# Sums of squares of queries and keys by two transfers of ScalarE instead of four of SyncE, and the first gates of the MLPs over both token runs side by side

## The chip, the cores and the metric

The kernel runs on one core of one Trainium2 chip. The metric is the device time of one execution in microseconds (us). TensorE (PE) multiplies matrices, with a weight load (PEld) beside each product; VectorE (DVE), ScalarE (ACT) and GpSimd (POOL) work on vectors; SyncE (SP) does nothing here but issue transfers (DMAs). An engine runs its instructions in their order: one that waits holds up all that stand behind it on that engine. ACT and POOL can issue transfers too, between their other instructions.

## The reference

A decoder of two layers over 528 tokens (16 learned ones ahead of 512), width 1024. Layer 0 is attention with a forget gate, layer 1 a gated linear recurrence (HGRN2), and each is followed by a gated MLP. What bears on the change:

```python
q, k, v, f_logit, o_gate = split(rms_norm(h) @ w_in)
q = rms_norm(q.reshape(B, L, 16, 64), q_gain) * 64 ** -0.5
k = rms_norm(k.reshape(B, L, 16, 64), k_gain)
p = softmax(where(causal, q . k + c_t - c_s, -inf))
o = (p @ v) * sigmoid(o_gate)
...
a = rms_norm(h) @ w_gate
a = conv_b + conv_w[0] * a[t - 2] + conv_w[1] * a[t - 1] + conv_w[2] * a[t]
y = (silu(a) * (rms_norm(h) @ w_up)) @ w_down
```

The mean squares in the change's name are those of `rms_norm(q)` and `rms_norm(k)`, one number for each token and head.

## The kernel before

Activations lie transposed, features on the partitions and tokens along the row, and the 528 tokens are cut into two runs of 264 (`full`). A product is made to float32 accuracy out of three products of halves: `proj_unit` gives for each tile of 128 features high weights by high input (L255), high weights by low input (L258), low weights by high input (L259). `weights` brings a 128x1024 block of weights by one SP transfer (L199), makes its high half on ACT (`hi`, L200) and its low half on DVE (`lo`, L126).

The program names what each engine has to do in Python generators (`fox` for the attention, `hgrn`, `ffn` for the MLPs), which `weave` steps in turn by the costs that they yield. A scheduler of the framework then orders the instructions of each engine by a simulated timeline, and puts in the waits. So an edit in one place can shift the order around it on every engine.

The attention (`fox`) goes over eight pairs of heads. In one iteration four pairs are in work: `stage_a` of pair p+3, `stage_n` of p+2, `lse` of p+1, and the attending itself of pair p.

- `stage_a` projects queries and keys. ACT squares the sums (L540) and copies them scaled (L541). A product with `hsel` adds the squares over each head (L549), two heads by four groups of (query or key) by (run), into one bank. ACT copies it to `strow` (L550). Four SP transfers (L554) fold the eight rows of `strow` into `am2`, 64 partitions by 33, on which DVE works quickly: it adds `et`, the epsilon term of every token (L557), and takes the inverse root in ten operations (L343 to L347). Two transfers (L564) unfold the result into `rows`.
- `stage_n` spreads `rows` over the partitions with the table `sel` (L578, PE), multiplies queries and keys by it (L579, DVE), makes high and low halves, and packs them by six SP transfers a pair (`pack`, L605) into `pk` or `two`; `decays` adds rows of the forget gate by SP (L617).
- `lse` finds the softmax's maxima and sums, two heads a pair: scores on PE (L751, L752, L754), maxima on DVE (L764 to L772), sums on ACT (L119, `junk`), and the row `lrow` (L786 on PE, L788 on DVE, transfers L791 and L792).
- The attending makes the scores again (L808, L809), probabilities `pt` on ACT (L119), and their product with `v` (L823). In between PE does projections, the output gate's and the values' among them (L306 and others). Vector `tot` (L486) of the forget gate is needed by L488.

Ahead of the pairs, `et` is filled by four SP transfers (L440) from `ssr`, the mean squares of the tokens, which two equal rows hold.

In the MLPs `plain(j)` works on the first two blocks of 128 gates, m = 0 and 1, with the plain products (later blocks use another scheme). `ga` names its two token runs: (0, 264) and (264, 264) in the first MLP, (14, 256) and (270, 258) in the second. For each run `proj_unit` goes over eight tiles, and DVE multiplies the bank by the tokens' inverse norms into `A` (L1256).

```python
am2 = self.tiny.tile([64, 33], F32, name="am2", tag="am2")
for g in range(4):
    nc.sync.dma_start(
        am2[16 * g : 16 * g + 16, :], strow[32 * g : 32 * g + 2, :].rearrange("r (j c) -> r j c", c=33)
    )
nc.vector.tensor_tensor(am2, am2, et, ALU.add)
```

## Time and profile before

| | us |
| --- | --- |
| median of three runs (lowest to highest) | 1445.19 (1443.09 to 1445.87) |
| the profiled execution, its own time | 1447.99 |
| span of the profiled execution | 1446.2 |
| PE busy in it | 1417.7 |
| DVE busy | 1009.4 |
| ACT busy | 723.9 |

The profiled execution is 1.8 us above its span and 2.8 us above the median. PE is busy for 98% of the span, so the time is set by what PE has to do, by the clock that it is granted, and by the 28.5 us in which it does nothing. A row of a timeline gives start, duration and instruction, and in brackets the idle time just before it and what ended it. The attention lasts until some 376 us, the first MLP starts at 377 us, the second near 1110 us.

### The profile page before, as it was taken

What the parts mean: (1) busy time and instruction counts of PE and PEld (TensorE: products, weight loads), DVE (VectorE), ACT (ScalarE), POOL (GpSimd) and SP (SyncE); (2) the same over time, 40 slices, a digit from 0 to 9 for tenths busy, and PEclk for the clock granted to TensorE, in tenths of its full rate; (3) what the DMA queues carried; (4) which work ended last, traced back from release to release, by engine and by line L of the source; (5) the groups of instructions that cost most, each with busy time, mean ns of one, the idle gap of its engine ahead of it and who ended that gap; (6) DMA issues with size and microseconds to landing.
All of it is one profiled execution on the core that took longest, in us unless ns stands there. A gap on an engine that the chain in (4) does not pass through costs nothing.

```text
span 1446.2 us, 29795 instructions
## 1 busy us (share of the span) xinstructions
PE 1417.7 (98%) x11368; PEld 1336.7 (92%) x11368; DVE 1009.4 (70%) x2282; ACT 723.9 (50%) x1528; POOL 178.7 (12%) x309
## 2 busy tenths in 40 slices
PE   7999999999999999999999999999999999999998
PEld 7898878999999999999999999999999899999997
DVE  6546454776698876777776667687567887777774
ACT  5355555664566555454543323333345665555551
POOL 4000000000412222221000000000022222222100
PEclk9999999999999999999999999999999999999999
DMA  4424344422889898896321202212165899989733
GB/s 162 121 63 134 67 126 124 111 86 85 225 184 253 217 227 212 204 221 152 95 77 60 88 19 71 74 60 73 60 182 138 217 251 224 233 214 224 200 89 101
DMA packets 104311, 206.90 MB, mean 143 GB/s; under 512 B 14168, under 2 KB 18008, under 8 KB 104168
## 3 DMA queue, kind: packets, MB, share of 16 engines
q1 hardware_dynamic: 79688, 158.33, 35.5%
q0 software_dynamic: 24480, 46.67, 18.7%
q8 instruction: 89, 1.46, 0.4%
q14 instruction: 54, 0.44, 0.1%
HBM read 168.53 MB, written 2.10 MB: 118 GB/s over the span
## 4 chain that ended last, share of the span: by engine, by line
PE 92%; DMA 3%; DVE 2%; ACT 1%; SPq 1%; issue 1%; ACTq 0%; DVEq 0%
PE psp L255 7%; PE psp L258 7%; PE psp L259 7%; PE pss L255 7%; PE pss L258 7%; PE pss L259 7%; PE psp L306 6%; PE psp L1192 5%; PE psp L1194 5%; PE psp L1193 5%; PE psd L1192 3%; PE psd L1193 3%; PE psd L1194 3%; PE psc L823 2%; PE pss L981 1%; PE psc L1192 1%
## 5 line engine op out<-in xcount | busy, mean ns | idle before, releaser
L126 DVE TENSOR_TENSOR lo<-raw,hi 128x512 fp32r<-128x512 f32 (+2 forms) x322 | 253.4, 791 | 86.4 <-ACT hi L1169 46.9
L255 PE MATMUL psp<-xhi,hi 128*128 128x264 f32 (+2 forms) x784 | 227.1, 290 | 6.1 <-ACT xhi L331 6.1
L258 PE MATMUL psp<-xlo,hi 128*128 128x264 f32 (+2 forms) x784 | 225.6, 288 | 0.0
L259 PE MATMUL psp<-xhi,lo 128*128 128x264 f32 (+2 forms) x784 | 225.1, 288 | 0.0
L1169 ACT CAST hi<-raw 128x512 fp32r<-128x512 f32 (+1 forms) x232 | 139.0, 604 | 171.2 <-PE pss L258 53.9
L258 PE MATMUL pss<-room,hi 128*128 128x264 f32 (+2 forms) x532 | 169.7, 320 | 0.0
L259 PE MATMUL pss<-room,lo 128*128 128x264 f32 (+2 forms) x532 | 168.9, 320 | 0.0
L255 PE MATMUL pss<-room,hi 128*128 128x264 f32 (+2 forms) x532 | 168.3, 320 | 0.0
L255 PEld LDWEIGHTS psp<-xhi,hi 128*128 128x128 f32 x784 | 148.9, 190 | 9.3 <-ACT xhi L331 6.1
L200 ACT CAST hi<-raw 128x1024 fp32r<-128x1024 f32 (+2 forms) x86 | 83.2, 968 | 146.0 <-PE psp L258 71.5
L258 PEld LDWEIGHTS psp<-xlo,hi 128*128 128x128 f32 x784 | 148.8, 190 | 2.0 <-issue 1.9
L259 PEld LDWEIGHTS psp<-xhi,lo 128*128 128x128 f32 x784 | 148.2, 189 | 2.0 <-issue 1.9
L1192 PE MATMUL psp<-xhi,hi 128*128 128x264 f32 (+1 forms) x480 | 136.5, 284 | 3.1 <-ACT hi L1169 2.3
L1194 PE MATMUL psp<-xhi,lo 128*128 128x264 f32 (+1 forms) x480 | 136.3, 284 | 0.7 <-DVE lo L126 0.5
L1193 PE MATMUL psp<-xlo,hi 128*128 128x264 f32 (+1 forms) x480 | 135.8, 283 | 0.0
L1169 ACT CAST hi<-two 128x512 fp32r<-128x512 f32 x118 | 72.9, 619 | 83.8 <-PE psd L1193 31.7
L259 PEld LDWEIGHTS pss<-room,lo 128*128 128x128 f32 x532 | 100.1, 189 | 6.3
L258 PEld LDWEIGHTS pss<-room,hi 128*128 128x128 f32 x532 | 100.2, 188 | 5.2
L255 PEld LDWEIGHTS pss<-room,hi 128*128 128x128 f32 x532 | 99.5, 188 | 4.2
L1316 DVE TENSOR_TENSOR h<-h,pss 128x264 f32<-128x264 f32 (+2 forms) x145 | 73.5, 510 | 35.8 <-PE pss L259 35.4
L1192 PEld LDWEIGHTS psp<-xhi,hi 128*128 128x128 f32 x480 | 90.7, 189 | 6.2 <-ACT hi L1169 3.7
L1192 PE MATMUL psd<-xfhi,hi 128*128 128x264 f32 (+1 forms) x320 | 91.1, 285 | 3.2 <-ACT psd L1205 1.7
(489 smaller groups left out, 3958.9 us busy)
## 6 DMA issues: line engine op xcount, KB each, us to landing
raw<-gu SPq DMA_DIRECT2D x136, 256.0 KB
two<-gu SPq DMA_DIRECT2D x102, 256.0 KB
raw<-dn SPq DMA_DIRECT2D x80, 256.0 KB
two<-gu POOLq DMA_DIRECT2D x74, 256.0 KB, 6.4
one<-gu SPq DMA_DIRECT2D x40, 256.0 KB
two<-two POOLq DMA_DIRECT2D x40, 256.0 KB, 4.8
pk<-stg SPq DMA_DIRECT2D x30, 264.0 KB
raw<-wqk SPq DMA_DIRECT2D x14, 512.0 KB
```

The source lines that it names most:

```text
L126: self.nc.vector.tensor_tensor(out, x, y, ALU.subtract)
L200: nc.scalar.copy(hi, raw)
L255: ins = mm(ps, hi[:, i, :], xh, start=k == 0, stop=False)
L258: mm(ps, hi[:, i, :], xl, start=False, stop=False)
L259: mm(ps, lo[:, i, :], xh, start=False, stop=k == total - 1)
L306: mm(ps[:tn, :256], y[:, t0 : t0 + tn], w, start=n == 0, stop=n == 23)
L823: ins = mm(o, v[:, j, 2 * (p % 2) + hd, :], w[hd][0], start=j == 0, stop=j == last)
L1169: nc.scalar.copy(hi, raw)
L1192: mm(ps, hi[:, k, :], xh, start=start and k == 0, stop=False, skip_group_check=not start)
L1193: mm(ps, hi[:, k, :], xl, start=False, stop=False, skip_group_check=not start)
L1194: mm(ps, lo[:, k, :], xh, start=False, stop=k == 3, skip_group_check=not start)
L1316: nc.vector.tensor_tensor(hv, hv, ps, ALU.add)
```

## The change

Two parts. In the sums of squares ACT itself issues two transfers behind its copy to `strow` (L555 of the changed file), the first for the first row of each of the four groups (one head of the pair), the second for the second row, 32 partitions each. With that the rows of `am2` stand in another order (first by head, then by group), and so `et` is filled from one of the equal rows of `ssr` in each of its four transfers, and the table `sel` is written for the new order. In the MLPs `plain` steps the products of both runs together, two tiles of one and then two of the other, and multiplies both banks after. Sizes, the number of products and all other transfers stay. In the changed file the lines of the attention from L441 on stand one lower (L557 is L556, L605 is L604, L788 is L787); L199, L200, L255 keep their numbers.

```diff
--- before.py
+++ after.py
@@ -435,8 +435,7 @@
             mm(sr[:2, :tn], self.onesd, self.ss[:, t0 : t0 + tn], start=True, stop=True)
             nc.vector.tensor_copy(ssr[:, t0 : t0 + tn], sr[:2, :tn])
         for g in range(4):
-            t0, tn = full[g % 2]
-            nc.sync.dma_start(et[16 * g : 16 * g + 16, :], ssr[:, t0 : t0 + tn].rearrange("r (j c) -> r j c", c=33))
+            nc.sync.dma_start(et[16 * g : 16 * g + 16, :], ssr[0:1, :].rearrange("r (j c) -> r j c", c=33))
         nc.vector.tensor_scalar(et, et, EPS, EPS, ALU.add, ALU.mult)
         self.spread_rs(rs, SEG0, start)
         rcol = [0, 1, 2, 3, 5]
@@ -550,10 +549,10 @@
             nc.scalar.copy(strow, pst[:, :264])
             yield 0.9
             am2 = self.tiny.tile([64, 33], F32, name="am2", tag="am2")
-            for g in range(4):
-                nc.sync.dma_start(
-                    am2[16 * g : 16 * g + 16, :], strow[32 * g : 32 * g + 2, :].rearrange("r (j c) -> r j c", c=33)
-                )
+
+            four = strow.rearrange("(g r) (j c) -> g r j c", g=4, c=33)
+            for r in range(2):
+                nc.scalar.dma_start(am2[32 * r : 32 * r + 32, :], four[:, r, :, :])
             nc.vector.tensor_tensor(am2, am2, et, ALU.add)
             y = self.rsqrt(am2, "q")
             yr = self.tiny.tile([64, 2, 33], F32R, name="yr", tag="yr")
@@ -1250,9 +1249,12 @@
             A, t = new_pair("A"), new_pair("t")[:, :, :n]
             for m in range(2):
                 wg = [block(a[f"gu{layer}"][2 * j + m, 0, k]) for k in range(2)]
-                for t0, tn in ga:
-                    ps = self.bank("sp"[m])[:, :tn]
-                    yield from self.proj_unit(ps, wg, self.x, t0, tn)
+                banks = [self.bank("sp"[m])[:, :tn] for _, tn in ga]
+
+                units = [self.proj_unit(ps, wg, self.x, *t) for ps, t in zip(banks, ga)]
+                for costs in zip(*units):
+                    yield sum(costs)
+                for ps, (t0, tn) in zip(banks, ga):
                     nc.vector.tensor_tensor(A[:, m, 2 + t0 : 2 + t0 + tn], ps, self.rsb[:, t0 : t0 + tn], ALU.mult)
                 smooth(t[:, m, :], A[:, m, :], 2 * j + m)
                 input_forms(2 * m)
@@ -1428,7 +1430,8 @@
     o["lmask"] = lm
     sel = np.zeros((16, 4, P), np.float32)
     for r in range(16):
-        sel[r, r // 2 % 4, 64 * (r % 2) : 64 * (r % 2) + 64] = 1.0
+        i = r // 4 % 2
+        sel[r, r % 4, 64 * i : 64 * i + 64] = 1.0
     o["sel"] = sel
     return o
```

The scheduler orders the engines anew. What the prediction speaks of stands at three places.

SP around the fourth pair of heads. `pk` is the packed queries and keys, `am` the tile `am2`, `wqk` a block of projection weights. Before:

```order
L199 DMA raw<-wqk 128x1024 x2
L605 DMA pk_266<-stg 64x2x528 x2
L605 DMA pk_266<-stg 64x1056
L605 DMA pk_271<-stg 64x2x528 x2
L605 DMA pk_271<-stg 64x1056
L554 DMA am_1405<-strow 16x1x33 x4
L199 DMA raw<-wqk 128x1024
L617 DMA pk_248<-cneg 1x8x66 x2
```

And now:

```order
L791 DMA two<-lrow 2x16
L604 DMA pk_266<-stg 64x2x528 x2
L604 DMA pk_266<-stg 64x1056
L604 DMA pk_271<-stg 64x2x528 x2
L604 DMA pk_271<-stg 64x1056
L199 DMA raw<-wqk 128x1024 x2
L616 DMA pk_248<-cneg 1x8x66 x2
```

The two loads of weights stood ahead of the six packed transfers and now stand behind them; the transfers of `am` have left the queue.

DVE around the third pair. L557 (now L556) adds `et`, L343 to L347 are the inverse root, `lrow` is what PE's L751 waits for, `negm` are maxima. Before:

```order
L126 TENSOR_TENSOR lr_183<-ls,lr_183 128x5
L557 TENSOR_TENSOR am_1089<-am_1089,et 64x33
L343 TENSOR_SCALAR rqq<-am_1089 64x33
L345 TENSOR_TENSOR ruq<-rqq 64x33
L346 SCALAR_TENSOR_TENSOR ruq<-ruq,am_1089 64x33
L788 CAST lrow<-pss 10x128
```

And now:

```order
L556 TENSOR_TENSOR am_1085<-am_1085,et 64x33
L771 TENSOR_TENSOR negm<-negm 128x1
L343 TENSOR_SCALAR rqq<-am_1085 64x33
L345 TENSOR_TENSOR ruq<-rqq 64x33
L346 SCALAR_TENSOR_TENSOR ruq<-ruq,am_1085 64x33
L347 SCALAR_TENSOR_TENSOR rqq<-ruq,rqq 64x33
L775 TENSOR_TENSOR ssum<-ssum 128x1
```

The wait for `am` no longer stands ahead of `lrow`, which follows sixteen rows further down; it stands ahead of a maximum, `negm`.

ACT around the fourth pair's copy to `strow`; `pt` are probabilities that PE waits for. Before:

```order
L119 ACTIVATE junk,ssum<-pss,negm 128x400
L550 COPY strow<-psd 128x264
L200 CAST hi<-raw 128x1024
L119 ACTIVATE pt<-pss 128x144 x2
L119 ACTIVATE junk,ssum<-pss,negm 128x264 x2
```

And now:

```order
L119 ACTIVATE junk,ssum<-pss,negm 128x272
L549 COPY strow<-psd 128x264
L119 ACTIVATE pt<-pss 128x272
L555 DMA am_1399<-strow 32x1x33 x2
L119 ACTIVATE pt<-pss 128x272 x2
L119 ACTIVATE junk,ssum<-pss,negm 128x400
```

Two issues now stand among ACT's probabilities and sums, in this pair one instruction behind the copy; in the others they follow it directly or within three.

## Rows read from the trace of the kernel before

**Rows 1.** The page: busy time by engine (us, share, instructions), and the chain by engine

```profile
PE 1417.7 (98%) x11368; PEld 1336.7 (92%) x11368; DVE 1009.4 (70%) x2282; ACT 723.9 (50%) x1528; POOL 178.7 (12%) x309
...
PE 92%; DMA 3%; DVE 2%; ACT 1%; SPq 1%; issue 1%; ACTq 0%; DVEq 0%
```

**Rows 2.** The waits of DVE: waits for, total us, times, longest us

```profile
DVE am L557 <- DMA am<-strow: 23.9, 8, 6.2
```

**Rows 3.** Timeline of PE: start us, duration us, instruction, idle time before it, releaser

```profile
66.88 0.38 PE L488 MATMUL psc<-tot,cst 128*128 128x2 f32 x2 [1.62 <-DVE tot L486]
...
99.95 0.45 PE L751 MATMUL pss<-two 66*128 66x400 f32 x1 [1.86 <-DVE lrow L788]
...
188.06 0.45 PE L786 MATMUL pss<-identr,lr 128*128 128x128 f32 x1 [1.99 <-DVE rqq L347]
...
386.48 0.39 PE L255 MATMUL pss<-xhi,hi 128*128 128x264 f32 x1 [1.52 <-ACT xhi L331]
```

**Rows 4.** Windows: us, busy of PE, PEld, DVE, ACT, POOL, granted clock, DMA

```profile
101.00:102.00 1.00, 1.00 (x8) 0.89 (x7) 0.84 (x5) 0.92 (x3) 0.00 (x0) 0.56 0.02 4
102.00:103.00 1.00, 1.00 (x7) 1.00 (x7) 1.00 (x4) 0.35 (x1) 0.00 (x0) 0.50 0.00 0
...
104.00:105.00 1.00, 1.00 (x9) 1.00 (x8) 0.06 (x1) 0.90 (x4) 0.00 (x0) 0.74 0.06 8
188.00:189.00 1.00, 0.94 (x5) 0.97 (x6) 0.79 (x4) 0.00 (x0) 0.00 (x0) 0.50 0.97 381
...
193.00:194.00 1.00, 1.00 (x9) 1.00 (x8) 1.00 (x6) 0.02 (x1) 0.00 (x0) 0.86 0.02 4
```

**Rows 5.** The chain of waits, third pair: start us, us, what

```profile
90.82 0.54 SPq L605
...
94.08 1.20 SPq L554
...
97.11 1.68 DMA am<-strow
...
98.86 0.20 DVE am L557
...
99.95 0.45 PE pss L751
```

**Rows 6.** Timeline of SP's queue (its issues), fourth and sixth pair

```profile
113.38 0.81 SPq L199 DMA_DIRECT2D raw<-wqk  x2
115.27 6.37 SPq L605 DMA_DIRECT2D pk<-stg  x6
...
176.11 6.10 SPq L605 DMA_DIRECT2D two<-stg  x6
182.32 3.50 SPq L554 DMA_DIRECT2D am<-strow  x4
185.93 0.82 SPq L199 DMA_DIRECT2D raw<-wqk  x2
```

**Rows 7.** Timeline of ACT, third pair's copy and sixth pair's cast of weights

```profile
88.85 0.35 ACT L550 COPY strow<-psd 128x264 f32<-128x264 f32 x1
...
189.38 1.04 ACT L200 CAST hi<-raw 128x1024 fp32r<-128x1024 f32 x1 [3.63 <-DMA raw<-wqk]
```

**Rows 8.** The tile am: DMA issues, ns min/median/max, first and last start us

```profile
L554 SPq DMA_DIRECT2D am<-strow x32: 610/619/1723, 31.0 to 255.0; - x32
```

**Rows 9.** Windows of the attention: engines, granted clock, DMA share, GB/s

```profile
110.00:120.00 10.00, 10.00 (x76) 6.68 (x76) 6.55 (x15) 6.64 (x20) 0.00 (x0) 1.00 0.59 162
180.00:185.00 5.00, 4.54 (x24) 2.71 (x22) 2.40 (x8) 2.49 (x10) 0.00 (x0) 1.00 0.98 223
180.00:190.00 10.00, 7.55 (x46) 5.37 (x45) 5.05 (x25) 3.81 (x15) 0.26 (x2) 0.82 0.79 217
```

**Rows 10.** Timeline of DVE, sixth pair, with the idle time before it

```profile
187.01 0.18 DVE L557 TENSOR_TENSOR am<-am,et 64x33 f32<-64x33 f32 x1 [1.51 <-DMA am<-strow]
```

## The prediction

> **What bounds the kernel now.** I read the page first: PE is busy for 1417.7 of 1446.2 us, and 92% of the chain that ended last is PE's own work [rows 1]. The number of products doesn't change, so the change can win two things alone: part of the 28.5 us in which PE is idle, and full clock where less was granted. Next I read which idle time lies where the change works. DVE waits 23.9 us in eight waits, one for each pair of heads, for the folded sums `am` [rows 2]. DVE's waits cost nothing by themselves. But three of PE's longest waits end behind one of these eight: 1.62 us at 66.88, where PE waits for `tot`, 1.86 us at 99.95, where it waits for `lrow`, and 1.99 us at 188.06, where it waits for a row of the same inverse root or for `lr` beside it [rows 3]. In each case what PE wants was ready to be made and stood behind L557 on DVE. The chain of the third pair shows it from end to end: ACT copies `strow` from 88.85 to 89.20 [rows 7], but at that time SP is busy with other transfers; the first of four packed ones goes out at 90.82, the four for `am` from 94.08 to 97.1, they land 1.68 us later, L557 runs at 98.86, and PE gets `lrow` at 99.95 [rows 5]. So 9.7 us go by between the end of the copy and L557, and only 1.7 of them are the transfer's own landing.
>
> The clock comes last. After the wait at 99.95 the granted clock is 0.56, 0.50, 0.50 and 0.74 in the four windows from 101 to 105, and after the wait at 188.06 it is 0.50 from 188 on and 0.86 in the last window, 193 to 194 [rows 4]; 0.50 is the lower of the two levels, 1.2 instead of 2.4 GHz. After the waits of 1.62 and 1.52 us [rows 3] no window shows less than full clock. The loss is 0.44 + 0.50 + 0.50 + 0.26 = 1.70 us at the first place, and 4.94 us at half plus 0.14, so 2.6 us, at the second.
>
> **The sums of squares: what goes.** Four issues a pair leave SP, 3.50 us in the sixth pair [rows 6], and what they stood behind there, six packed transfers of 6.1 to 6.4 us [rows 6], no longer delays them. Two issues a pair come to ACT. No row shows an issue by ACT. The nearest is SP's issue of the same data, 610 to 1723 ns with a median of 619 [rows 8]; I take 0.65 us, near the median because ACT's queue is empty, and keep 1.72 as the upper end. From the copy to L557 it is then 0.35 + 2 x 0.65 + 1.68 = 3.3 us (2.9 to 5.5) instead of 9.7. In the new order 84, 62 and 66 matmuls lie in the second, third and sixth pair between the copy's inputs and the first product that depends on something behind L556. At 76 in 10 us [rows 9], 0.13 us each, that is 11, 8 and 9 us, more than 5.5. So all three waits should go, at either price: 1.62 + 1.86 + 1.99 = 5.5 us, and with the last two the clock's 1.70 + 2.6 = 4.3 us. Together **9.8 us**. Late next at 188 would be the weights: their load is issued at 185.93 and the cast of their high half starts at 189.38 [rows 6, 7]. But that load stood behind the four issues that leave, and moves ahead by 3.5 us with them.
>
> **What comes new.** First the fourth pair. Before, its loads of weights were issued at 113.38, ahead of six packed transfers at 115.27 [rows 6]; now they stand behind them (first place of the order above). From the release of the six it takes 6.1 us of issues [rows 6], 0.2 of the load's own, 3.45 until it has landed and 1.04 for the cast [rows 6, 7]: 10.75 us. Between the same release and the first product with these weights the new order has 61 matmuls. At 0.13 us that is 8.0 us, at the pace of the slow stretch, 46 in 7.55 us [rows 9], 10.0. The shortage is 0.75 to 2.75 us; the low half is made after the high one and covers itself only in part, so I take **2.1 us**, and 0 to 4 as bounds. Second the eighth pair, where only 34 matmuls, 4.4 us, lie between the copy and the first product behind L556. From the copy to L557 it is 3.3 us, and on to PE about 1.1 (98.86 to 99.95 in the third pair [rows 5], 187.01 to 188.06 in the sixth [rows 3, 10]), together 4.4: no cover is left. I take **1.0 us** (0 to 2.5). Third, in the third pair L556 now stands ahead of a maximum on which ACT's sums wait, **0.3 us** (0 to 1). The fifth and seventh pair keep 51 and 57 matmuls, 6.7 us and more, and the first has 92; nothing is counted there.
>
> ACT gets 16 x 0.65 = 10.4 us of issues within some 225 us (31 to 255 [rows 8]) in which it is busy for about two thirds (6.64 of 10 us [rows 9]); what hides them is the distance from ACT's `pt` to PE's use of it. I count 0; the bound is in the rivals. For `et` four transfers stay four; 0, at most one issue of 0.6 us either way [rows 8].
>
> **The MLPs' gates.** The first product of the third tile waits 1.52 us for its input at 386.48 [rows 3]. Before, 13 matmuls were ahead of it in this block, now 15, since the second run's first tiles go first; at 0.13 us that is 0.3 us. In the second MLP the multiplication into `A` comes later and the input forms on DVE move; no row shows what that does, and I bound it by two thirds of the first MLP's wait, 1.0 us either way, and take 0. So **-0.3 us**.
>
> **The sum.** -9.8 + 2.1 + 1.0 + 0.3 - 0.3 = -6.7 us. The profiled execution took 1447.99 us, so the same execution would take 1441.3; it lies 2.8 us above the median of 1445.19, and against the median the forecast is **1438.5 us**.
>
> **Rivals.** (a) *New waits give it back.* The four places above take their upper ends: 4 us in the fourth pair and, since that is longer than 1.86, a fall of the clock of 2.6 as after 188.06 [rows 4], 2.5 in the eighth, 1.0 in the third: 10.1 us against 10.1 gained. The time would be 1445.2. For it speaks that the order of the fourth pair builds just the queue that cost 1.99 us at 188.06; against it that this needs every pace at its end.
>
> (b) *The small transfers are as late as before.* By this SP's queue was not the cause, and packets of the packed transfers hold up those of `am`, whoever issues them. In the fourth pair both are now released within a few matmuls of each other. If `am` lands only when the six are through, 6.1 us [rows 6] instead of 1.68, the fourth and eighth pair stop PE for 4.4 us each and then run at half clock, 2.2 us each as the mean of the two places: 13.2 in place of 3.1, so -6.7 + 10.1 = +3.4, 1448.6. Against it stands that in the sixth pair, while the DMA engines were busy for 0.98 of the stretch from 180 to 185 [rows 9], L557 ran at 187.01 [rows 10], 1.2 us after the four issues that began at 182.32 and took 3.50 [rows 6]. The Trainium skill speaks for it: its page "DMA: Bandwidth & Descriptors", section "Issuing engines are not separate DMA queues", says that transfers started by the scalar, sync or gpsimd engine run on the same 16 DMA engines and interleave, and that starting them from several engines saves only the sequencer's issue time, usually small beside the transfer. In this trace the waiting in SP's queue, about 8 of 9.7 us, is the larger part, so here the time saved by that very rule would not be small; whether ACT's packets wait among the packed ones no run yet shows.
>
> (c) *ACT stands still at its own issues.* This is the one that ends slower most clearly. In the fourth pair `pt` stands right behind the two issues, and PE uses it 21 matmuls later, 2.8 us at 0.13 us each. Of these 0.4 go for `pt` itself, so the point that decides is an issue of 1.2 us. At 1.72 [rows 8] the two take 3.4, PE is short by 1.0 us a pair, 8 us in all, and where this meets another wait the clock falls too, twice as before, 4.3 us: -6.7 + 12.3 = +5.6, 1450.8. Against it: the median issue is half of the deciding one, and the long ones came on a queue full of other transfers.
>
> **How the numbers follow.** The forecast, with its terms at any value that leaves a gain above 3 us, has 0.66; (a) 0.17, (b) 0.07, (c) 0.10. The smallest difference that runs of this kernel tell from none is about 0.2%, 2.9 us. All of the forecast's case is faster. Of (a) I give 0.03 to faster, 0.11 to no difference, 0.03 to slower; of (b) 0.02 to no difference and 0.05 to slower; of (c), whose price falls with the issue, 0.01, 0.04 and 0.05. That makes 0.70, 0.17 and 0.13. The range: with no new wait at all and the second MLP at its better end it is -9.8 - 0.3 - 1.0 = -11.1, 1434.1; at the upper end it takes in case (a) with the second MLP's 1.0, 1446.2. Outside are most of (b) and (c).
>
> **What would show it.** Right: no issue for `am` on SP; two on ACT at 0.6 to 0.8 us each; L557's eight waits (now L556) shrunk from 23.9 us to under 10; no idle of PE over 1 us at the three places, full clock there. A new idle of 1 to 3 us before a product of the fourth pair, released by ACT's cast of weights, and one of about 1 us in the eighth. The first MLP's wait at 1.3 us. Wrong: a landing of `am` of over 3 us, issues on ACT of over 1.2 us with PE waiting for `pt`, or half clock after the fourth pair. The sum itself fails if PE's idle time falls by 5 us or more and the time stays; then products would have become slower.

## The result, and the profile after

The changed kernel is slower. Its median is **1451.15 us** (1448.51 to 1454.62, seven runs) against 1444.81 us (1443.06 to 1446.44) of the kernel before beside it: a ratio of **1.0044 [1.003, 1.0057]**, so 0.44% or 6.3 us, outside the interval but small. The forecast was 1438.5 us, faster, in a range of 1434.1 to 1446.2. The time lies above the range, and the sign is wrong.

What the change was to take away is gone. The page of the profiled execution after (1451.15 us), beside [rows 1], and the tile `am`, beside [rows 2, 8]:

```profile
PE 1423.8 (98%) x11368; PEld 1338.2 (92%) x11368; DVE 1009.1 (70%) x2282; ACT 722.5 (50%) x1528; POOL 179.2 (12%) x309
```

```profile
L555 ACTq DMA_DIRECT2D am<-strow x16: 532/561/1501, 31.5 to 239.5; - x16
...
DVE am L556: 11.1, 6
```

DVE's waits for the folded sums fell from 23.9 to 11.1 us, ACT's issues take a median of 0.56 us (all sixteen together 12.4 us, 0.78 on average, since one of the two takes 1.1 to 1.5 us in five of the pairs), and in PE's timeline none of the three waits at `tot`, `lrow` and `lr` of [rows 3] is left. But PE is busy for 6.1 us longer with the same number of matmuls, so the loss is not idle time in the main: products became slower. The windows of the attention tell where. Here are those of the kernel before (us; busy time and instructions of PE, PEld, DVE, ACT, POOL; granted clock; DMA share; GB/s; the windows from 110 and 180 stand in [rows 9]):

```profile
60.00:70.00 10.00, 8.38 (x69) 8.17 (x68) 5.25 (x24) 3.34 (x6) 0.00 (x0) 1.00 0.63 174
100.00:110.00 10.00, 10.00 (x71) 9.38 (x71) 5.96 (x27) 6.23 (x21) 0.21 (x2) 0.83 0.02 4
120.00:130.00 10.00, 9.78 (x83) 8.99 (x82) 5.21 (x26) 4.81 (x15) 0.23 (x2) 1.00 0.69 162
190.00:200.00 10.00, 10.00 (x71) 9.56 (x71) 7.21 (x21) 7.06 (x22) 0.21 (x2) 0.84 0.34 111
```

And these are the same windows after:

```profile
60.00:70.00 10.00, 10.00 (x85) 10.00 (x84) 7.55 (x33) 5.24 (x9) 0.00 (x0) 1.00 0.88 226
...
100.00:110.00 10.00, 10.00 (x82) 8.95 (x80) 5.60 (x19) 5.04 (x17) 0.21 (x2) 1.00 0.01 2
110.00:120.00 10.00, 7.96 (x63) 4.81 (x62) 5.21 (x20) 4.98 (x18) 0.00 (x0) 0.98 0.72 155
120.00:130.00 10.00, 9.86 (x47) 8.41 (x47) 5.13 (x20) 4.98 (x17) 0.26 (x2) 0.51 0.60 180
180.00:190.00 10.00, 10.00 (x75) 6.89 (x74) 5.79 (x23) 4.67 (x11) 0.00 (x0) 1.00 0.66 188
190.00:200.00 10.00, 10.00 (x88) 9.55 (x88) 6.70 (x19) 5.43 (x20) 0.23 (x2) 1.00 0.52 160
```

Read the x behind PE's busy time. The second, third and sixth pair do 11 to 29 matmuls more in 10 us than before, at full clock. The fourth pair (110 to 130) does 110 instead of 159, and for ten of its twenty microseconds at a clock of 0.51, the lower of the two levels. Its timelines show how it comes to that. First SP's queue after, beside [rows 6]: six packed transfers and then the two loads of weights, the other way round than before.

```profile
111.47 6.13 SPq L604 DMA_DIRECT2D pk<-stg  x6
117.68 2.51 SPq L199 DMA_DIRECT2D raw<-wqk  x2
```

Then ACT and DVE, where the two issues take 2.07 us, the sums land 3.1 us after the second has ended (4.6 after it began), and L556 stands ahead of the masks of L811:

```profile
112.86 2.07 ACTq L555 DMA_DIRECT2D am<-strow  x2
...
118.05 0.19 DVE L556 TENSOR_TENSOR am<-am,et 64x33 f32<-64x33 f32 x1 [2.14 <-DMA am<-strow]
...
119.03 0.28 DVE L811 TENSOR_TENSOR pss<-pss,cst 128x128 f32<-128x128 f32 x1
```

Then PE, whose product at 119.69 waits for a `pt` behind such a mask; the first product with the loaded weights is the one at 124.75:

```profile
119.69 0.38 PE L807 MATMUL pss<-pk 98*128 98x16 f32 x1 [2.04 <-ACT pt L119]
...
120.68 1.79 PE L822 MATMUL psc<-pt,v 128*64 128x272 f32 x12
...
124.75 0.59 PE L255 MATMUL psp<-xhi,hi 128*128 128x264 f32 x1
```

In the kernel before the first of these dense products starts at 118.34, between the small ones of the attention:

```profile
118.34 0.28 PE L255 MATMUL psp<-xhi,hi 128*128 128x264 f32 x1
```

So three things come together in the fourth pair after: a wait of 2.04 us, an order in which the dense products of the projections (L255 to L259) come later, and half clock for some ten microseconds from 119.6 on. Which of them is the cause, the experiments have to tell.

For a ledger I counted matmuls in PE's timeline and took the time from the start of one to the start of the other, in us. Between the same counts nearly the same work is done. Beside the kernel before stands the one with the gates' part alone (e3 below), which has the same attention as before: it shows by how much one execution differs from another.

| matmuls of the attention | before | e3 | after |
| --- | --- | --- | --- |
| 250 to 750 (second and third pair) | 66.0 | 64.4 | 62.0 |
| 750 to 950 (fourth pair) | 25.4 | 25.2 | 32.0 |
| 950 to 1250 | 37.7 | 37.8 | 38.5 |
| 1250 to 1450 (sixth pair) | 29.8 | 30.9 | 24.9 |
| 1450 to 1750 | 38.1 | 38.1 | 37.4 |
| 1750 to 1950 (eighth pair) | 25.5 | 25.5 | 28.7 |
| 1950 to 2750 | 99.9 | 100.2 | 102.9 |

Against e3 the gains are 2.4 + 6.0 = 8.4 us, near the forecast's 9.8. The losses are 6.8 in the fourth pair and 3.2 + 2.7 from the eighth on, 12.7 us where the forecast had 3.4; between these places it is 0.7 more once and 0.7 less once. The 6.8 us of the fourth pair are about the wait of 2.04 us and half of the ten microseconds at half clock.

### The profile page after: what moved, and what is told of

Same layout as the page of the kernel before. It is cut to its first block, busy times and chain, and to the rows that moved or that the text cites. A ratio compares the mean times of both kernels' runs of the same rounds, so it can differ in the third digit from the quotient of the medians.

```text
span 1449.4 us, 29757 instructions
## 1 busy us (share of the span) xinstructions
PE 1423.8 (98%) x11368; PEld 1338.2 (92%) x11368; DVE 1009.1 (70%) x2282; ACT 722.5 (50%) x1528; POOL 179.2 (12%) x309
## 5 line engine op out<-in xcount | busy, mean ns | idle before, releaser
L255 PE MATMUL psp<-xhi,hi 128*128 128x264 f32 (+2 forms) x784 | 227.4, 291 | 6.5 <-ACT xhi L331 6.1
L259 PE MATMUL psp<-xhi,lo 128*128 128x264 f32 (+2 forms) x784 | 226.6, 290 | 0.0
L259 PE MATMUL pss<-room,lo 128*128 128x264 f32 (+2 forms) x532 | 168.9, 320 | 0.0
L255 PE MATMUL pss<-room,hi 128*128 128x264 f32 (+2 forms) x532 | 168.2, 320 | 0.0
L255 PEld LDWEIGHTS psp<-xhi,hi 128*128 128x128 f32 x784 | 149.4, 191 | 11.9 <-ACT xhi L331 6.1
L200 ACT CAST hi<-raw 128x1024 fp32r<-128x1024 f32 (+2 forms) x86 | 83.2, 968 | 144.8 <-PE psp L258 72.1
L259 PEld LDWEIGHTS psp<-xhi,lo 128*128 128x128 f32 x784 | 149.1, 190 | 2.0 <-issue 1.4
L259 PEld LDWEIGHTS pss<-room,lo 128*128 128x128 f32 x532 | 100.1, 189 | 6.3
L258 PEld LDWEIGHTS pss<-room,hi 128*128 128x128 f32 x532 | 100.2, 188 | 5.2
L255 PEld LDWEIGHTS pss<-room,hi 128*128 128x128 f32 x532 | 99.5, 188 | 4.2
L126 DVE TENSOR_TENSOR lo<-two,hi 128x512 fp32r<-128x512 f32 x118 | 81.1, 688 | 16.1 <-ACT hi L1168 13.5
```

The source lines that it names most:

```text
L126: self.nc.vector.tensor_tensor(out, x, y, ALU.subtract)
L200: nc.scalar.copy(hi, raw)
L255: ins = mm(ps, hi[:, i, :], xh, start=k == 0, stop=False)
L258: mm(ps, hi[:, i, :], xl, start=False, stop=False)
L259: mm(ps, lo[:, i, :], xh, start=False, stop=k == total - 1)
```

## The experiments

Ratios are to the kernel before, which ran beside each of them; 1.0044 is the changed kernel's own. The experiments ran on several chips, so kernels of different groups are compared by these ratios. The expectations speak of theories: A holds L556 ahead of the masks for the cause, B the issues on ACT, C the clock's fall at 24 us, D the place of the loads of weights in SP's queue.

**The parts apart (e2, e3).** e2 is the changed kernel with the gates as before:

```diff
-                banks = [self.bank("sp"[m])[:, :tn] for _, tn in ga]
...
-                for costs in zip(*units):
-                    yield sum(costs)
+                for t0, tn in ga:
+                    ps = self.bank("sp"[m])[:, :tn]
+                    yield from self.proj_unit(ps, wg, self.x, t0, tn)
```

> The changed kernel with the MLPs' first gates run after run as before; the attention's order is the changed kernel's on every engine. Theories A and B: slower than before by 5 to 8 us, with PE's wait of 2 us in the fourth pair and half clock after it. If the gates were the cause: faster than before by 3 us or more.

Measured: 1450.51 us, 1.0041 [1.0026, 1.0055]. e3 is the kernel before with the gates side by side, the same lines the other way round.

> The kernel before with the gates side by side alone; the attention's order is that of before on every engine. Theories A and B: 0.5 to 2.5 us faster than before (in the changed kernel the distance to before shrank from 5.4 us at the first MLP to 3.2 at the end), and the three waits of PE in the attention stay. If the gates were the cause of the loss: slower by 4 us or more.

Measured: 1444.06 us, 0.9993 [0.998, 1.0005]. The loss belongs to the sums of squares; the gates' part is within the measurement.

**The wait in the fourth pair (e1).** In the changed kernel L556 of this pair, and what follows from it, is placed behind the last mask:

```diff
+            def finish():
+                add = nc.vector.tensor_tensor(am2, am2, et, ALU.add)
+                if p == 3:
+                    self.after(add, self.masked)
...
+            if p == 3:
+                held.append(finish)
```

> The changed kernel, but in the fourth pair DVE's addition of et (L556) and the inverse root are placed behind the last masks of the attending (L811); up to that place every engine has the changed kernel's order. Theory A (in the fourth pair L556 waits on DVE for a transfer that lands late, the masks stand behind it, PE stops for 2.04 us at 119.69 and then runs at half clock until 129.6, 4.8 us): that wait of PE goes, and the time falls by 2 to 7 us against the changed kernel, to 1444 to 1449; less than 6.8 if the weights of the next pair, loaded behind six packed transfers, are what is late next. Theory B (ACT stands still at its own two issues, 2.07 us there): nothing changes, 1450 to 1452, since ACT's issues stay. Theory C (the clock's fall at 24 us, behind the 3.08 us wait for the first norms, is what costs): nothing changes on average, and the fall at 24 us is there in this profile or not by chance.

Measured: 1451.55 us, 1.005 [1.0035, 1.0065]. The edit did what it should: the wait of 2.04 us became one of 0.62. The time stayed. PE's timeline of e1 shows what is late next, and the windows that the clock falls all the same, after no wait longer than 0.67 us:

```profile
115.88 0.28 PE L817 MATMUL pss<-pk 98*128 98x16 f32 x1 [0.62 <-ACT pt L119]
118.33 0.45 PE L795 MATMUL pss<-identr,lr 128*128 128x128 f32 x1 [0.67 <-DVE ruq L345]
122.42 0.59 PE L255 MATMUL psp<-xhi,hi 128*128 128x264 f32 x1 [1.91 <-ACT hi L200]
```

```profile
118.00:119.00 1.00, 0.67 (x4) 0.70 (x5) 0.89 (x6) 0.00 (x0) 0.01 (x1) 0.50 0.94 209
119.00:120.00 1.00, 1.00 (x7) 1.00 (x7) 0.00 (x0) 0.00 (x0) 0.00 (x0) 0.50 0.92 348
```

So the wait behind L556 falls as the cause. The fourth pair takes 32.0 us as in the changed kernel: the 2.04 us are gone, and 1.91 us before the first dense product, for the cast of the late weights, have come in their place. What is left is the stretch without dense products.

**ACT as the issuer (e4, e12).** e4 is the changed kernel with its two transfers issued by SP:

```diff
-                nc.scalar.dma_start(am2[32 * r : 32 * r + 32, :], four[:, r, :, :])
+                nc.sync.dma_start(am2[32 * r : 32 * r + 32, :], four[:, r, :, :])
```

> The changed kernel, but its two transfers a pair are issued by SyncE, not ScalarE; the order of the attention comes out another way from the second pair on. Theory B: without issues on ACT the loss against before goes, 1440 to 1444. Theory A: the time goes with whether L556 has to wait ahead of something that PE needs; with two issues instead of four in SP's queue behind the packed transfers the waits of DVE are some 1 to 2 us shorter than in the kernel before, and the time is between 1440 and 1447. Theory C: the fall at 24 us is there or not by chance here too.

Measured: 1446.25 us, 1.0012 [1.0, 1.0025], 4.6 us below the changed kernel by the ratios. In this kernel the loads of the fourth pair stand ahead of its packed transfers again, so it alone doesn't tell the issuer from the order. e12 is the kernel before with two issues a pair added on ACT, of the same data into a tile that nobody reads:

```diff
+            spare = self.tiny.tile([64, 33], F32, name="spare", tag="spare")
+            four = strow.rearrange("(g r) (j c) -> g r j c", g=4, c=33)
+            for r in range(2):
+                nc.scalar.dma_start(spare[32 * r : 32 * r + 32, :], four[:, r, :, :])
```

> The kernel before, with its four SP transfers a pair for am, and beside them the changed kernel's two ACT transfers a pair, from the same rows into a spare tile that nobody reads. The attention's order comes out another way from the second pair on. Theory B (ACT's own issues stop PE): 4 us or more slower than before. Theory D (what counts is where the loads of weights stand against the packed transfers, and the bare stretches that follow): within 3 us of before either way, and PE's waits, where there are any, do not begin behind ACT's two issues.

Measured: 1448.03 us, 1.0035 [1.0019, 1.005], some 5 us slower: the total that theory B gave, not D's. The scheduler's order moves in this kernel too. Its profiled execution, 1444.51 us, is the fastest of its twelve and shows no wait of PE behind an issue. It gains 5.0 us on before in the sixth pair and loses 4.3 in matmuls 1450 to 1750, where PE waits 1.37 us at 200.98 for late weights and runs at half clock from 201 to 208, and 2.3 after the eighth pair. Where the 5 us of the median go stays open, and e12 doesn't speak against B.

**The place of the loads in SP's queue (e5, e6).** e5 is the kernel before, with the fourth pair's loads of weights held until its packed transfers are issued. Nothing else in it is the change's:

```diff
+                if p == 4:
+                    self.after(self.load, self.packed)
```

> The kernel before, but the two loads of weights of the fourth pair's stretch have to be issued behind the six packed transfers of that stretch, as in the changed kernel; every order is that of before up to there, and again from the next pair but one. Theory D (the products with those weights are the dense work that fills the attention's stretch of small products and waits; where the loads stand behind the packed transfers these products come after that stretch, which then runs bare, slowly, and at half clock): 5 to 9 us slower than before, 1450 to 1454, with half clock somewhere from 115 to 130 us. Theory A (L556 ahead of the masks): within 1.5 us of before, since L557 is still issued by SP and no mask is moved.

SP's timeline of e5 has the order asked for, PE's has two new waits, and the windows a bare fourth pair:

```profile
112.65 6.09 SPq L607 DMA_DIRECT2D pk<-stg  x6
...
122.53 0.35 SPq L199 DMA_DIRECT2D raw<-wqk  x1
```

```profile
125.08 0.58 PE L810 MATMUL pss<-two 98*128 98x256 f32 x1 [3.16 <-ACT junk L119]
127.27 0.59 PE L255 MATMUL psp<-xhi,hi 128*128 128x264 f32 x1 [1.40 <-ACT hi L200]
```

```profile
110.00:120.00 10.00, 9.07 (x74) 5.66 (x73) 5.43 (x20) 5.39 (x21) 0.23 (x2) 1.00 0.59 129
120.00:130.00 10.00, 5.43 (x29) 4.71 (x29) 5.55 (x23) 4.01 (x11) 0.00 (x0) 0.74 0.48 143
```

Matmuls 750 to 950 take 34.1 us instead of 25.4. Measured in all: 1445.85 us, 1.0018 [1.0007, 1.0028], only 2.2 us above the median beside it and below theory D's range. In its profile the order behind this place moved as well, and the sixth pair's loss disappeared (25.8 us in place of 29.8 for matmuls 1250 to 1450).

e6 does the reverse in the changed kernel: the second head's packed transfers wait for the issue of the loads in the fourth pair.

```diff
+                    for o, i in moves:
+                        x = dma(o, i)
+                        if load is not None:
+                            self.after(x, load)
...
+                if hd and p in DEFER:
+                    deferred.append(move)
```

> The changed kernel, but the second head's three packed transfers of the fourth pair's stretch wait for the issue of the two loads of weights; the sums of squares stay on ACT. Theory D: 5 to 8 us faster than the changed kernel, 1443 to 1446, no half clock from 115 to 130 us. Theory A: 0 to 2 us faster, 1449 to 1451, if L556 still stands ahead of masks.

The windows of e6 show the fourth pair mended, and the eighth slower:

```profile
120.00:130.00 10.00, 10.00 (x86) 9.30 (x86) 7.89 (x18) 7.25 (x20) 0.00 (x0) 1.00 0.18 55
...
240.00:250.00 10.00, 7.66 (x24) 4.10 (x24) 3.77 (x19) 4.26 (x11) 0.00 (x0) 0.61 0.32 112
250.00:260.00 10.00, 10.00 (x59) 9.08 (x59) 4.82 (x16) 2.63 (x11) 0.23 (x2) 0.71 0.18 56
```

Matmuls 750 to 950 take 28.1 instead of 32.0 us, matmuls 1750 to 1950 take 33.2 instead of 28.7. The time is 1448.54 us, 1.0035 [1.0022, 1.0048], above theory D's range.

Over all kernels of the study the fourth pair splits without an exception by the order of these loads. Ahead of the packed transfers (in e6 and e8 of the second head's), matmuls 750 to 950 take 25.1 to 28.1 us (before, e3, e4, e6, e8, e9, e10, e11, e12, e15, e17), behind them 31.6 to 34.1 (after, e1, e2, e5, e7, e13, e14, e16, e18). ACT's issues are on both sides (e6 and e8 on the first, e5 and e13 without them on the second). Half clock goes with it: each of the nine late ones has 6.8 to 10.3 us of it in this stretch, and of the eleven others only e8 has any, 1.7 us.

The sixth pair shows that the order by itself isn't the point but how late the loads go out. After, its loads stand behind packed transfers too, as SP's timeline has it:

```profile
177.36 3.52 SPq L604 DMA_DIRECT2D two<-stg  x4
181.31 2.01 SPq L199 DMA_DIRECT2D raw<-wqk  x2
```

Yet the pair is fast: they go out 3.3 us behind its first matmul, number 1250. Before, behind the six packed transfers and the four of `am` [rows 6], it was 14.0 us. The profiles of all twenty kernels split by this delay in the three pairs:

| pair | loads go out, us behind its first matmul | us for its matmuls | kernels with half clock in it |
| --- | --- | --- | --- |
| fourth (750 to 950) | 0.2 to 4.5, 11 kernels | 25.1 to 28.1 | 1 of 11 |
| | 8.5 to 16.3, 9 kernels | 31.6 to 34.1 | 9 of 9 |
| sixth (1250 to 1450) | 0.1 to 8.5, 12 kernels | 24.7 to 28.3 | 0 of 12 |
| | 13.3 to 14.5, 8 kernels | 29.6 to 35.0 | 7 of 8 |
| eighth (1750 to 1950) | -3.9 to 0.5, 9 kernels | 25.2 to 26.5 | 0 of 9 |
| | 2.5 to 7.2, 11 kernels | 27.3 to 33.2 | 8 of 11 |

So the change's gain in the sixth pair and its losses in the fourth and eighth go with one thing, the time at which the weights' loads go out. For the fourth and the eighth pair e5, e6 and e7 move it on purpose; for the sixth no run does. Within a group the delay doesn't order the times, least of all in the eighth pair, where loads at 3.0 us go with 33.2 us in e6 and with 27.7 in e7.

**The eighth pair (e7, e8).** After, SP's loads of weights stand there behind both heads' packed transfers too. SP's timeline after:

```profile
237.52 2.10 SPq L604 DMA_DIRECT2D pk<-stg  x3
...
243.20 2.06 SPq L604 DMA_DIRECT2D pk<-stg  x3
245.36 2.42 SPq L199 DMA_DIRECT2D raw<-wg  x2
```

e7 is e6's edit in the eighth pair alone, `DEFER` (6,) instead of (2,).

> The changed kernel, but in the eighth pair's stretch the second head's three packed transfers wait for the issue of the loads of the gate's weights; all orders are the changed kernel's up to there, the fourth pair included. Theory D: 2 to 4.5 us faster than the changed kernel, 1446.5 to 1449. If the loss in the eighth pair were ACT's own waiting (its two issues take 2.0 us there): within 1 us of the changed kernel.

SP's timeline of e7 has the loads between the two heads:

```profile
235.53 2.09 SPq L607 DMA_DIRECT2D pk<-stg  x3
...
241.32 0.81 SPq L199 DMA_DIRECT2D raw<-wg  x2
242.19 2.51 SPq L607 DMA_DIRECT2D pk<-stg  x3
```

Measured: 1444.52 us, 1.0006 [0.9996, 1.0016], as fast as the kernel before and 5.5 us below the changed one by the ratios, more than theory D gave. Matmuls 1750 to 1950 take 27.7 instead of 28.7 us and 1950 to 2750 take 99.8 instead of 102.9; the fourth pair keeps its 31.9. So 4.1 us of the 5.5 are at the place of the edit and behind it; the rest isn't placed. With both pairs mended (e8, `DEFER` (2, 6)) it should be better still:

> Both of the two last edits at once, the changed kernel with the loads ahead in the fourth and the eighth pair. Theory D: 7 to 12 us faster than the changed kernel, 1439 to 1444, so as fast as before or faster. Theories A and B: 1447 to 1450.

It wasn't: 1447.0 us, 1.0026 [1.0016, 1.0035]. The order moves again and PE has a new wait of 2.36 us for `rows` at 249.55. Beside e7's profile the fourth pair takes 4.7 us less, the second and third 1.8 more, matmuls 1450 to 1750 2.7 more and the eighth pair 1.5 more.

**What the three old waits were worth (e9, e10, e11).** e9 is the kernel before with L557 placed behind `tot`, `lrow` and `lr` in the second, third and sixth pair, so that nothing PE wants stands behind it; e10 does it in the sixth alone, e11 adds the gates to e9.

```diff
+        held, BEHIND = [], {1: "tot_made", 2: "lrow_made", 5: "lr_made"}
...
+                if p in BEHIND:
+                    self.after(add, getattr(self, BEHIND[p]))
```

> The kernel before with its four SP transfers a pair, but DVE's addition of et is placed behind what PE waited for at the three places of the prediction: behind tot in the second pair, behind lrow in the third, behind lr in the sixth. Theory P (the prediction's first term: these three waits cost 5.5 us and up to 4.3 us of clock, and go without a new loss): 5 to 9 us faster than before, 1435 to 1439. Theory Q (the time saved at such a wait is mostly lost at the next place where PE has only small dependent products): 0 to 3 us faster, with new waits or half clock further on in the attention.

> The kernel before with the addition placed behind lr in the sixth pair alone; nothing else moves but some 40 rows on DVE and a few on PE and SP there. Theory P: the wait of 1.99 us at 188 us goes and with it 2.6 us of half clock, 3 to 5 us faster, 1439 to 1441. Theory Q: the next wait there is for the weights, whose cast of the high half started at 189.38 (PE needed them at 190.9): 0 to 1.5 us faster and half clock still there.

> The three placements and the gates side by side together, the order of the attention that of the first kernel of this call. The two parts should add: the first kernel's time less 0.5 to 2 us. Theory P: 1433 to 1438; theory Q: 1440 to 1443.

Measured: e9 1445.84 us, 1.0014 [1.0003, 1.0025]; e10 1444.07, 1.0003 [0.999, 1.0017]; e11 1445.14, 1.0013 [0.9999, 1.0027]. Taking the waits away by themselves gains nothing. In e9's profile the second and third pair take 2.4 us less than in e3, and matmuls 950 to 1950 take 1.8 more than there. PE's timeline of e10 shows why in the sixth pair: 1.99 us are gone, 1.21 stand at the weights a little later, whose loads go out as late as before. And its windows have the half clock of the sixth pair without the wait that I had held for its cause:

```profile
182.91 0.28 PE L819 MATMUL pss<-pk 98*128 98x16 f32 x1 [0.27 <-ACT pt L119]
189.43 0.59 PE L255 MATMUL psp<-xhi,hi 128*128 128x264 f32 x1 [1.21 <-ACT hi L200]
```

```profile
180.00:181.00 1.00, 1.00 (x6) 0.34 (x6) 0.43 (x1) 0.14 (x1) 0.00 (x0) 1.00 0.86 258
...
184.00:185.00 1.00, 0.98 (x12) 0.81 (x8) 0.61 (x5) 0.32 (x3) 0.23 (x2) 0.62 0.10 19
185.00:186.00 1.00, 0.89 (x5) 0.92 (x6) 0.32 (x3) 0.00 (x0) 0.00 (x0) 0.50 0.40 105
186.00:187.00 1.00, 1.00 (x6) 0.88 (x7) 1.00 (x7) 0.00 (x0) 0.00 (x0) 0.50 0.88 348
```

In the profile of the kernel before, too, the clock falls while that wait has just begun (PE stands from 186.07 to 188.06), not at its end:

```profile
186.00:187.00 1.00, 0.07 (x4) 0.00 (x0) 0.00 (x0) 0.00 (x0) 0.00 (x0) 0.72 0.30 31
```

**The same shift of the order in both kernels (e13 to e18).** If the order decides and not the transfers' issuer, the change's worth must itself depend on the order. Three numbers that steer `weave` were shifted, each in the kernel before and in the changed one:

```diff
-            yield 0.9
+            yield 2.0
...
-                (chain(*fill), 0.97 * cost),
+                (chain(*fill), 1.05 * cost),
...
-                (stage_t(p) if p >= 0 else None, 8.5),
+                (stage_t(p) if p >= 0 else None, 7.5),
```

> The kernel before with another step behind the copy to strow (2.0 instead of 0.9), which only steers the weaving: another order from the fourth pair on, in which six packed transfers of the fourth pair stand ahead of the loads of weights. Theory D: slower than before by 2 to 6 us in the fourth pair, as far as no other wait goes with it. Theory B: as before, within 2 us, since no issue is on ACT.

> The changed kernel with the same shift. The loads still stand behind the packed transfers in the fourth and eighth pair. Theory D: as the changed kernel, 4 to 7 us above before, and no more than 3 us above the shifted kernel before. Theory B: 4 to 6 us above the shifted kernel before.

> The kernel before with the projections' share of the weaving at 1.05 instead of 0.97 of their cost: another order from the second pair on, loads of weights mostly ahead of or between the packed transfers. Theory D: within 2 us of before. Theory B: the same.

> The changed kernel with the same shift; in its order the loads stand behind packed transfers in the fourth, sixth and eighth pair. Theory D: 4 to 8 us above the shifted kernel before, by bare stretches of PE there. Theory B: 4 to 6 us above the shifted kernel before; the two theories differ here in the place, fourth and eighth pair against every pair alike.

> The kernel before with the attending's share of the weaving at 7.5 instead of 8.5: another order from the third pair on; the loads stand ahead in the fourth pair and behind eight or nine packed transfers in the later ones. Theory D: 2 to 5 us slower than before. Theory B: within 2 us of before.

> The changed kernel with the same shift; the loads stand behind the packed transfers in the fourth pair and the later ones. Theory D: 4 to 8 us above before, and above the shifted kernel before by 1 to 5 us, by the fourth pair alone. Theory B: 4 to 6 us above the shifted kernel before.

| shift | before, us | after, us | after less before |
| --- | --- | --- | --- |
| none | 1444.81 | 1451.15 | +6.3 |
| `yield` behind the copy, 0.9 to 2.0 (e13, e14) | 1448.7, 1.0031 [1.0019, 1.0044] | 1447.36, 1.0021 [1.001, 1.0032] | -1.3 |
| cost of the filling, 0.97 to 1.05 (e15, e16) | 1443.04, 0.9996 [0.9986, 1.0006] | 1446.54, 1.0019 [1.0009, 1.0029] | +3.5 |
| attending, 8.5 to 7.5 (e17, e18) | 1471.74, 1.0206 [1.0186, 1.0227] | 1466.31, 1.0159 [1.0146, 1.0173] | -5.4 |

I had expected the third shift to cost a few microseconds; it cost the kernel before 28. The change's own worth runs from 5.4 us of gain, in that much slower order, to 6.3 of loss; the -1.3 of the first shift is within its intervals. So theory B's 4 to 6 us of loss in every order falls. A smaller price of the issues, hidden under gains of the order, isn't excluded. The first shift also shows the late loads without any edit at the transfers: in e13, a kernel before, the loads of the fourth pair come behind its packed transfers, the pair takes 32.5 us, and its window is

```profile
120.00:130.00 10.00, 6.55 (x41) 5.58 (x41) 5.45 (x24) 4.87 (x18) 0.23 (x2) 0.60 0.64 179
```

Theory D named the places and often missed the totals: beside e5, e6, e7, e8 and e12 also those of e14, e16, e17 and e18 lie outside what it gave.

## Why the prediction was wrong

**What goes** came out in size and only in part as a mechanism. The three waits are gone after, their half clock with them, and the sections around them are 8.4 us shorter than in e3. But the waits were not a gain to be had by themselves: e9 and e10 took them away and won nothing. In the sixth pair the gain of 6.0 us goes with the loads of weights, which left the queue 3.3 us behind matmul 1250 instead of 14.0; the prediction had that move down as a guard against a next wait and put the price on the wait for `lr` and the clock behind it. The half clock there comes without that wait too (e10), so the agreement of 8.4 with 9.8 is partly luck. The third pair's share was partly one execution's: the wait of 1.86 us and the fall of the clock [rows 3, 4] are 0.27 us and none in e3, whose attention is ordered as before. The sum then took all 6.7 us off a median that lay 2.8 us under that very execution, as if the median held the same waits. ACT's issue was estimated at 0.65 us; the median was 0.56 and the mean 0.78.

**What comes new** is the step that failed, by its price: 2.1 us were put down for the fourth pair, as a wait for the late weights with full clock behind it, and the pair lost 6.8. The place was right, weights behind six packed transfers, and so was the wait's size: in e1, where PE has waited for hardly anything else ahead of them, it is 1.91 us, in e5 1.40. In the changed kernel itself it doesn't show, since PE has stood 2.04 us for `pt` by then. What the term left out is the rest of the stretch. The shortage of 0.75 to 2.75 us was counted in matmuls at an even pace of 0.13 us, with a slow one of 46 in 7.55 us that left out PE's idle time (those 46 took 10 us [rows 9]). But the late weights take the dense products out of the stretch, and the small ones that are left are slower: 47 in 10 us instead of 83, at half clock. e5 shows it in the kernel before, where the loads' place alone takes the fourth pair from 25.4 to 34.1 us; there PE is busy for 5.43 of 10 us. The eighth pair had 1.0 us, for sums without cover, and cost 3.2, with 2.7 behind it; e7, which only brings the loads there ahead of the second head's packed transfers, takes away 4.1 of these 5.9 and brings the whole kernel back to the time before.

The third pair's 0.3 us show nowhere, since PE has no wait there after. The MLPs' -0.3 us is neither confirmed nor refuted: the first MLP's wait at 386.48 fell from 1.52 to 0.30 us, where 1.3 were forecast, but PE then waits for `A` in that MLP, as its timeline after shows, and e2, whose gates stand as before, has no wait there either. e3 puts the whole at -0.8 us, inside the measurement.

```profile
395.42 0.39 PE L255 MATMUL pss<-xhi,hi 128*128 128x264 f32 x1 [0.30 <-ACT xhi L331]
...
410.71 0.36 PE L255 MATMUL pss<-xhi,hi 128*128 128x264 f32 x1 [1.26 <-DVE A L1258]
```

**The rivals.** (a), that new waits give the gain back with a fall of the clock in the fourth pair, was nearest in mechanism (4 + 2.6 us there against 6.8 measured), and its 0.17 was too little: it asked for a wait above 1.86 us to bring the clock down, and e1 shows the fall after none over 0.67. (b) was right of the landing: from the start of the last issue it took 3.1 to 4.6 us in the second, fourth, sixth and eighth pair, each time amid packed transfers, where the third pair before had 1.68 [rows 5]. (That 1.68 runs from the issue's start, so the 3.3 us from the copy to L556 counted the issue twice; in the fourth pair they became 5.6 all the same.) By the Trainium skill's page "DMA: Bandwidth & Descriptors", section "Issuing engines are not separate DMA queues", transfers of all issuers interleave on the same engines; the trace agrees, with these 3.1 to 4.6 us. But it was no cause of the loss, for with L556 out of the way the time stayed (e1). (c) was right of the issues in part, since three of them took more than its 1.2 us (1.26 to 1.50). As the cause it fell with e7, which keeps all sixteen issues and is as fast as the kernel before, and with the third shift, where the kernel with these issues is the faster one.

**What stays open.** Why mending both pairs (e8) is slower than mending the eighth alone: its profile shows where the time goes, not why the order costs it. Where e12's 5 us go, and with it whether the issues on ACT have a small price of their own. And why the changed kernel takes 2.7 us more from the eighth pair on, where PE has hardly a wait and full clock.

## What to carry to other kernels

Where a scheduler orders the queues, a transfer that leaves a queue moves everything behind it: read the new order for the loads of dense work that fills a chain of small dependent products, and how much later than that chain they go out, and price a late load by the pace of that stretch without its filling, clock included, not by the wait alone. Compare a wait over two executions before it enters a sum, and don't take its removal off a median that lies below the execution in which it was seen. Where orders can shift, move one steering number in both kernels by the same amount: if the difference changes its sign, as here between -5.4 and +6.3 us, it is a property of the order and not of the change alone.

## What the runs showed of the hardware that was not expected

The granted clock fell to its lower level with PE hardly idle: in e10 it is 1.00 until 184 us, 0.62 from 184 to 185 and 0.50 from 185 on. In the six microseconds ahead, 178 to 184, PE did small products of the attention, 4 to 8 matmuls in each, and stood idle for 0.5 us in all, never for more than 0.27 at a time. And the fall comes and goes for the same instructions. e9's profile has it in the sixth pair from 186 to 193, after no wait over 0.43 us; e11's, with the same attention, doesn't. At the start, where PE's instructions are the same in all these kernels, the changed kernel's profile has it from 24 to 31 us and the profile before doesn't:

```profile
23.00:31.00 8.00, 7.64 (x59) 6.11 (x60) 5.96 (x29) 2.94 (x8) 0.00 (x0) 1.00 0.17 61
```

This is the window of the kernel before, and the next one that after:

```profile
23.00:31.00 8.00, 7.73 (x33) 4.60 (x34) 5.53 (x27) 2.15 (x7) 0.00 (x0) 0.57 0.17 60
```

The first 220 matmuls take 35.7 us after and 32.7 before, a difference that belongs to no edit: e4's profile shows no fall there, e3's does. The wait ahead of it was 3.08 us in the profile after and 2.27 in the one before, but e7's profile has the fall after 2.27 as well.
